# A two-layer decoder trunk in float32: one 512-column matmul for the high part of a weight in the up projections

## The chip, the cores and the metric
One core of a Trainium2 chip runs the whole program in one launch. The metric is the device time of one execution in microseconds (us); smaller is better. TensorE multiplies, VectorE (DVE in the profile) and ScalarE (ACT) do the elementwise work, GpSimd (POOL) nearly nothing here, and SyncE (SP) issues the DMAs.

## The reference
256 tokens of width 2048 pass two layers in float32. Each layer is `x <- LN(alpha*x + mixer(x))`, then `x <- LN(alpha*x + ConvFFN(x))`. The mixer of layer 0 is stick-breaking attention (8 heads of 128) beside RWKV-7 time mixing (16 heads of 64); that of layer 1 is gated linear attention (4 heads). The part that is changed is the feed-forward network:

```python
def conv_ffn(x, w_up, conv_w, conv_b, w_down):
    gate, up = jnp.split(x @ w_up, 2, axis=-1)          # 2048 -> 2 x 5632
    gate = causal_depthwise_conv(gate, conv_w) + conv_b # three taps along the tokens
    h = jax.nn.gelu(gate, approximate=False) * up
    return h @ w_down                                   # 5632 -> 2048
```

## The kernel before
Every product is made from float32r operands: a float32 number is split in a high part (its cast to float32r) and a low part (what is left), and a product is high x high + high x low + low x high, three matmuls that add up in one PSUM accumulator.

Weights come from HBM as granules of 128 x 512 (`Stream`): one DMA brings two, ScalarE casts the high part (line 56) and VectorE subtracts it from the raw weight for the low part (line 57). The split granules wait in a ring of tiles (four, with up to four more in some stages). TensorE's order is the order in which the program is written; the other engines' orders are set by a scheduler that knows dependencies and priorities, weights first.

There are two kinds of product. `gemm_b` (lines 180 to 188) keeps a weight tile of 128 x 128 in the array and streams 256 tokens past it: the accumulator holds 128 features x 256 tokens. A granule holds four k tiles of one feature tile, so four granules, 48 matmuls of 256 columns, make one feature tile. `gemm_a` (lines 192 to 197) keeps the activations in the array and streams 512 weight columns: the accumulator holds 128 tokens x 512 features. The mixers' input projections are mostly `gemm_b` by way of `tile_b`, the output and down projections `gemm_a` by way of `block_a` and `proj_out`. `wave` makes the first four feature tiles of a projection at once, because the normed activations come only piece by piece.

Accumulators come from two pools of four PSUM banks: `g` for the projections (4 buffers of one bank, line 115), `t` for the rest. One bank holds 512 float32 numbers a partition. `tile_b` uses half of a bank; in the up projection gate and up of a pair p share one bank.

What reads an accumulator depends on the place. In layer 0 `shift` reads it twice, on ScalarE (line 548) and on VectorE (line 549), for the RWKV tiles r, k and v; q and k of the attention are copied by ScalarE (lines 942, 944). In layer 1 `q_post` and `k_post` read it on VectorE (lines 1079, 1090, 1093), `gate` on ScalarE (line 1179, shown as line 157). `residual` reads the blocks of `proj_out` on VectorE (line 302). In the up projection `finish` does the convolution, the GELU and the product with up (lines 453 to 460). Work beside the products, such as the attention itself, runs in generators that take a step every few granules (`tick`).

The tile of the input is `[128, 2, 256]`: the high parts of one k tile for all tokens, then the low parts.

Of the kernel before, what the change touches and what calls it, by code (L numbers as in the profile page):

```python
# [18 lines left out]
# how many granules the steps of the work beside the products lie apart  # L19
# [3 lines left out]
class Stream:  # L23
    """Weight granules [128, 512] in the order of use, split into two float32r parts."""
# [7 lines left out]
    def ahead(self):  # L32
        """split the first four granules before those of the stream before have been used"""
        K = self.K
        K.wpos = 0
        self.ready = [self.make() for _ in K.wbase]
# [27 lines left out]
class Kern:  # L64
# [14 lines left out]
    # Work beside the products: a generator that yields the number of granules to let pass  # L79
    # before its next step.  # L80
# [28 lines left out]
    def pools(self, ctx):  # L109
        tc = self.tc  # L110
        e = ctx.enter_context
        self.cst = e(tc.tile_pool(name="cst", bufs=1))
        self.xp = e(tc.tile_pool(name="xp", bufs=16))
        self.sm = e(tc.tile_pool(name="sm", bufs=2))
        self.psg = e(tc.tile_pool(name="psg", bufs=4, space=bass.MemoryType.PSUM))
        self.pst = e(tc.tile_pool(name="pst", bufs=4, space=bass.MemoryType.PSUM))
# [4 lines left out]
    def wpools(self, ctx, n, nraw, nw):  # L121
        """weights arrive n granules at a time"""
# [5 lines left out]
    def wextra(self, ctx, n, start=0):  # L128
        """room for n more granules as long as ctx is open"""
# [6 lines left out]
    def rsqrt(self, x, y, t):  # L136
        """y = x^-1/2 by exp(-ln(x)/2) and one step of Newton; t is scratch"""
# [7 lines left out]
    # The table sets of ScalarE are loaded where act_set says: what needs a table is issued  # L145
    # behind its load, and a load behind what needs the set before it.
# [16 lines left out]

    def g(self, shape=(P, 512)):
        return self.psg.tile(list(shape), F32, tag="g", name=f"g{self.uid()}")
# [4 lines left out]
    def split(self, dst, src, eng_hi="act"):  # L170
        """dst [128, 2, n] float32r <- src in two parts"""
# [7 lines left out]
    # out[f, tok] += W[k, f] x[k, tok]; a granule holds 4 k tiles of one feature tile  # L179
    def gemm_b(self, ps, w, xT, kg):  # L180
        nc = self.nc
        for j in range(4):
            k = kg * 4 + j
            wh, wl = w[:, 0, j * P:(j + 1) * P], w[:, 1, j * P:(j + 1) * P]
            nc.tensor.matmul(ps, lhsT=wh, rhs=xT[k][:, 0], start=k == 0, stop=False)  # L185
# [4 lines left out]
    # out[tok, n] += x[k, tok] W[k, n], both in two float32r parts; a granule holds 512 columns  # L190
    # of one k tile
# [7 lines left out]
    # out[tok, n] += x[k, tok] W[k, n]; a granule holds 512 columns of one k tile  # L199
    def wave(self, st, xT, made=None, first=False):  # L200
        """four feature tiles at once, k outside; made: steps that give 2 k tiles each"""
        nc = self.nc
        ps = [self.g((P, S)) for _ in range(4)]
# [5 lines left out]
        def mm(a, w, k, part=None):  # L209
            j = k % 4  # L210
            wh, wl = w[:, 0, j * P:(j + 1) * P], w[:, 1, j * P:(j + 1) * P]
            if part != 1:
                nc.tensor.matmul(ps[a], lhsT=wh, rhs=xT[k][:, 0], start=k == 0, stop=False)  # L213
                nc.tensor.matmul(ps[a], lhsT=wl, rhs=xT[k][:, 0], start=False, stop=False)  # L214
            if part != 0:
                nc.tensor.matmul(ps[a], lhsT=wh, rhs=xT[k][:, 1], start=False, stop=k == KT - 1)  # L216
# [22 lines left out]
        return ps  # L239
# [7 lines left out]
    def block_a(self, st, xs):  # L247
        """512 columns, both halves of the tokens"""
# [9 lines left out]
    def proj_out(self, xs, st, done, then=None, tail=4, after=None):  # L258
        """xs: (high, low) halves per k tile and token half; done(m, nb, ps, columns)"""
        nc = self.nc  # L260
        n = len(xs)
        for nb in range(4):
# [5 lines left out]
            # the first half of the tokens ends ahead of the second, and that in two parts  # L268
# [64 lines left out]
    def norm_out(self, h, g_d, b_d, out):  # L333
        """the last norm: a job before the sums are complete, that gives what follows each half"""
# [4 lines left out]
        # the blocks of each half that ScalarE and GpSimd take  # L339
# [24 lines left out]
    def norm(self, h, stats, gcol, bcol, g_d, b_d, lp, bp, then):  # L364
        """h^T of the normed h in two float32r parts. Returns the tiles, the steps that give two
        of them each, and a job that ends the norm of h itself."""
# [71 lines left out]
    def ffn(self, h, stats, ln, st, down_d, cw_d, then=None, last=None):  # L438
        """cw [128, 44, 4]: three taps and the bias of each feature"""
        nc = self.nc  # L440
        with ExitStack() as ctx:
# [10 lines left out]
            def finish(p, g, u):  # L452
                c = cw[:, p]
                t = ft.tile([P, S], F32, tag="ct", name=f"ct{self.uid()}")
# [7 lines left out]
            ps = self.wave(st, xT, made)  # L462
            finish(0, ps[0], ps[1])
            finish(1, ps[2], ps[3])
            self.spawn(late)
            for p in range(2, NFF):
                ps = (self.t if p < 4 else self.g)((P, 2, S))
                for a in range(2):
                    for kg in range(4):
                        self.gemm_b(ps[:, a], st.next(), xT, kg)  # L470
                finish(p, ps[:, 0], ps[:, 1])
# [6 lines left out]
# host side: layout only  # L478
def gran_b(np, W, cols):
    """[n, 128, 4, 512]: per feature tile (128 columns from cols[i]), its 16 k tiles"""  # L480
# [8 lines left out]
def wave(np, g):  # L489
    """the first four tiles [4, 128, 4(kg), 512] with the k groups outside"""  # L490
# [5 lines left out]
def gran_a(np, W):  # L496
    """[nb * K/512, 128, 4, 512]: per 512 columns, its k tiles"""
# [33 lines left out]
class Mix0:  # L531
    """In-projection of layer 0, stick-breaking attention and RWKV-7 time mixing."""
# [18 lines left out]
    def run(self, xT, made, win_b, win_v, win_qk, lw_d, g2_d, open_h, outer):  # L551
# [6 lines left out]
        with ExitStack() as ctx:  # L558
# [101 lines left out]
            def k_post(p, k):  # L660
# [6 lines left out]
                # the norm's guard; the factor 2^20 keeps ln in its range  # L667
# [735 lines left out]
```

## Time and profile before

| | |
|---|---|
| time of three runs | 2438.54, 2439.29, 2439.73 us (median 2439.29) |
| span of the profiled execution | 2437.5 us (the page gives no time beside it) |
| TensorE busy | 2405.3 us, 99%, 17770 matmuls |
| VectorE busy | 1554.8 us, 64% |
| ScalarE busy | 1301.8 us, 53% |
| mean granted TensorE clock | 0.991 of full speed |
| matmuls of `gemm_b` from tiles x, of 256 columns (lines 185 to 187) | 3 x 3024 |

The page's busy time counts a matmul from its start to its end, 282 ns for one of 256 columns, though the next one starts long before; how often one starts in a stretch says what it costs. The up projection of layer 0 runs from about 600 to 1030 us, that of layer 1 from about 1700 to 2170; the mixer of layer 0 fills the first 440 us, that of layer 1 lies between 1300 and 1680 us with its output projection.

### The profile page before, as it was taken

Reading aid. Unit: us, or ns where it says so; the run is one execution under the profiler, and the core shown is the slowest. Engines: PE = TensorE matmul, PEld = TensorE weight load, DVE = VectorE, ACT = ScalarE, POOL = GpSimd, SP = SyncE. Lnnn points to the kernel's source line nnn. Section 1 sums busy time; section 2 is a strip of 40 time slices with the busy share of each in tenths; the row PEclk is TensorE's granted clock in tenths of the full one; section 3 lists DMA queues with packets and bytes.
Section 4 is the critical chain, followed back from the end, with each engine's and each line's share of the span. In section 5 each row is a group of like instructions: output and inputs, shape, how many; then the busy total and the mean of one; then the engine's idle time right before and its main releaser. Section 6 shows DMA issues by size and latency. Waiting matters only on the chain.

```text
span 2437.5 us, 44745 instructions
## 1 busy us (share of the span) xinstructions
PE 2405.3 (99%) x17770; PEld 2253.8 (92%) x17770; DVE 1554.8 (64%) x2847; ACT 1301.8 (53%) x2450; POOL 12.0 (0%) x14
## 2 busy tenths in 40 slices
PE   8999999999999999999999999999999999999997
PEld 7998988889999999988898998989999999998887
DVE  5887755677666666655558666667766666655555
ACT  6655555555555555544437555555555555554442
POOL 0000000000000000000000000000000000000001
PEclk9999998999999999999999999999999999999999
DMA  5444433656555555555555554564655555565553
GB/s 175 161 134 168 145 105 104 210 163 224 189 184 185 188 183 188 184 193 195 184 173 177 170 173 166 175 213 163 218 184 189 183 185 188 183 216 199 195 186 138
DMA packets 123698, 434.79 MB, mean 178 GB/s; under 512 B 13744, under 2 KB 14640, under 8 KB 123488
## 3 DMA queue, kind: packets, MB, share of 16 engines
q1 hardware_dynamic: 123488, 431.93, 52.7%
q8 instruction: 139, 2.28, 0.4%
q14 instruction: 71, 0.58, 0.1%
HBM read 429.77 MB, written 2.10 MB: 177 GB/s over the span
## 4 chain that ended last, share of the span: by engine, by line
PE 95%; DVE 3%; DMA 1%; ACT 1%; issue 0%; SPq 0%; DVEq 0%; ACTq 0%
PE g L185 17%; PE g L187 17%; PE g L186 17%; PE g L195 10%; PE g L196 10%; PE g L197 10%; PE t L197 1%; PE t L195 1%; PE t L196 1%; DMA raw<-w0b 1%; PE g L213 1%; PE g L216 1%; PE g L214 1%; PE t L185 1%; PE t L187 1%; PE t L186 1%
## 5 line engine op out<-in xcount | busy, mean ns | idle before, releaser
L57 DVE TENSOR_TENSOR w<-raw,w 128x512 fp32r<-128x512 f32 x1584 | 1080.1, 690 | 769.9 <-ACT w L56 766.4
L56 ACT CAST w<-raw 128x512 fp32r<-128x512 f32 x1584 | 965.6, 620 | 958.3 <-PE g L187 461.4
L185 PE MATMUL g<-x,w 128*128 128x256 f32 x3024 | 852.6, 282 | 0.0
L187 PE MATMUL g<-x,w 128*128 128x256 f32 x3024 | 852.1, 282 | 0.0
L186 PE MATMUL g<-x,w 128*128 128x256 f32 x3024 | 851.8, 282 | 0.0
L185 PEld LDWEIGHTS g<-x,w 128*128 128x128 f32 x3024 | 569.7, 188 | 0.2
L186 PEld LDWEIGHTS g<-x,w 128*128 128x128 f32 x3024 | 569.7, 188 | 0.3
L187 PEld LDWEIGHTS g<-x,w 128*128 128x128 f32 x3024 | 569.6, 188 | 0.0
L197 PE MATMUL g<-w,hT 128*128 128x512 f32 (+1 forms) x704 | 255.4, 363 | 0.0
L196 PE MATMUL g<-w,hT 128*128 128x512 f32 (+1 forms) x704 | 255.3, 363 | 0.0
L195 PE MATMUL g<-w,hT 128*128 128x512 f32 (+1 forms) x704 | 255.3, 363 | 0.0
L185 PE MATMUL g<-xi,w 128*128 128x256 f32 x608 | 179.2, 295 | 0.0
L187 PE MATMUL g<-xi,w 128*128 128x256 f32 x608 | 173.4, 285 | 3.0 <-DVE w L57 2.9
L186 PE MATMUL g<-xi,w 128*128 128x256 f32 x608 | 172.8, 284 | 0.0
L195 PEld LDWEIGHTS g<-w,hT 128*128 128x128 f32 x704 | 133.0, 189 | 20.7
L196 PEld LDWEIGHTS g<-w,hT 128*128 128x128 f32 x704 | 133.0, 189 | 20.5
L197 PEld LDWEIGHTS g<-w,hT 128*128 128x128 f32 x704 | 132.9, 189 | 20.5
L187 PEld LDWEIGHTS g<-xi,w 128*128 128x128 f32 x608 | 116.1, 191 | 3.8 <-DVE w L57 3.8
L185 PEld LDWEIGHTS g<-xi,w 128*128 128x128 f32 x608 | 116.2, 191 | 3.1 <-issue 1.5
L186 PEld LDWEIGHTS g<-xi,w 128*128 128x128 f32 x608 | 116.3, 191 | 0.8
L213 PE MATMUL g<-x,w 128*128 128x256 f32 x192 | 55.8, 298 | 0.0
L157 ACT ACTIVATE ct<-ct 128x256 f32<-128x256 f32 x88 | 36.8, 418 | 32.5 <-DVE ct L457 32.5
(316 smaller groups left out, 2852.2 us busy)
## 6 DMA issues: line engine op xcount, KB each, us to landing
raw<-up SPq DMA_DIRECT2D x352, 512.0 KB, 3.6
raw<-dn SPq DMA_DIRECT2D x176, 512.0 KB, 4.3
raw<-w0b SPq DMA_DIRECT2D x53, 512.0 KB, 3.6
raw<-w1b SPq DMA_DIRECT2D x40, 512.0 KB, 3.8
raw<-w0qk SPq DMA_DIRECT2D x32, 512.0 KB, 3.6
raw<-w0o SPq DMA_DIRECT2D x32, 512.0 KB, 4.2
raw<-w1v SPq DMA_DIRECT2D x32, 512.0 KB, 3.6
raw<-w1o SPq DMA_DIRECT2D x32, 512.0 KB, 4.4
```

Source lines behind the costliest of these rows:

```text
L56: i = nc.scalar.copy(out=w[:, 0], in_=src).ins
L57: K.split_ins = nc.vector.tensor_sub(out=w[:, 1], in0=src, in1=w[:, 0].bitcast(F32)).ins
L157: i = self.nc.scalar.activation(out=out, in_=in_, func=func, **kw).ins
L185: nc.tensor.matmul(ps, lhsT=wh, rhs=xT[k][:, 0], start=k == 0, stop=False)
L186: nc.tensor.matmul(ps, lhsT=wh, rhs=xT[k][:, 1], start=False, stop=False)
L187: nc.tensor.matmul(ps, lhsT=wl, rhs=xT[k][:, 0], start=False, stop=k == KT - 1)
L195: nc.tensor.matmul(ps, lhsT=xh, rhs=w[0], start=first, stop=False)
L196: nc.tensor.matmul(ps, lhsT=xh, rhs=w[1], start=False, stop=False)
L197: nc.tensor.matmul(ps, lhsT=xl, rhs=w[0], start=False, stop=last)
L213: nc.tensor.matmul(ps[a], lhsT=wh, rhs=xT[k][:, 0], start=k == 0, stop=False)
L214: nc.tensor.matmul(ps[a], lhsT=wl, rhs=xT[k][:, 0], start=False, stop=False)
L216: nc.tensor.matmul(ps[a], lhsT=wh, rhs=xT[k][:, 1], start=False, stop=k == KT - 1)
```

## The change
In the up projections the accumulator of a feature tile becomes a whole bank of 512 columns. The high part of a weight tile meets the high and the low part of x in one matmul of 512 columns: the first 256 columns of the bank collect high x high, the others high x low. The low part of the weight meets the high part of x in a matmul of 256 columns, into the first half. At the end `finish` copies the second halves of gate and up to SBUF with ScalarE and adds the first halves with VectorE, and works on that sum. In `wave` the first four k tiles still take three matmuls, because the low parts of x come later.

A pair (gate, up) now needs two banks. So the pool `g` is made of two tiles of two banks each. `g2` gives such a tile; `g`, which all other products use, gives one half of a tile and at the next call the other.

```diff
-        self.psg = e(tc.tile_pool(name="psg", bufs=4, space=bass.MemoryType.PSUM))
+        self.psg = e(tc.tile_pool(name="psg", bufs=2, space=bass.MemoryType.PSUM))
+        self.half = None
...
+    def g2(self):
+        self.half = None
+        return self.psg.tile([P, 2, 512], F32, tag="g", name=f"g{self.uid()}")
+
     def g(self, shape=(P, 512)):
-        return self.psg.tile(list(shape), F32, tag="g", name=f"g{self.uid()}")
+        if self.half is None:
+            t = self.g2()
+            self.half = t[:, 1]
+            b = t[:, 0]
+        else:
+            b, self.half = self.half, None
+        return b[:, 0:math.prod(shape[1:])]
...
     def gemm_b(self, ps, w, xT, kg):
+        wide = ps.shape[1] == 2 * S
...
+            if wide:
+                nc.tensor.matmul(ps, lhsT=wh, rhs=xT[k].rearrange("p a b -> p (a b)"), start=k == 0, stop=False)
+                nc.tensor.matmul(ps[:, 0:S], lhsT=wl, rhs=xT[k][:, 0], start=False, stop=k == KT - 1)
+                continue
...
     def wave(...):
+            if wide and part is None:
+                nc.tensor.matmul(ps[a], lhsT=wh, rhs=xT[k].rearrange("p a b -> p (a b)"), start=False, stop=False)
+                nc.tensor.matmul(ps[a][:, 0:S], lhsT=wl, rhs=xT[k][:, 0], start=False, stop=k == KT - 1)
+                return
...
-            def finish(p, g, u):
+            def finish(p, ps):
+                gu = ft.tile([P, 2, S], F32, tag="gu", name=f"gu{self.uid()}")
+                if isinstance(ps, list):
+                    for i in range(2):
+                        nc.scalar.copy(out=gu[:, i], in_=ps[i][:, S:])
+                        nc.vector.tensor_add(out=gu[:, i], in0=ps[i][:, 0:S], in1=gu[:, i])
+                else:
+                    nc.scalar.copy(out=gu, in_=ps[:, :, S:])
+                    nc.vector.tensor_add(out=gu, in0=ps[:, :, 0:S], in1=gu)
+                g, u = gu[:, 0], gu[:, 1]
...
             for p in range(2, NFF):
-                ps = (self.t if p < 4 else self.g)((P, 2, S))
+                ps = [self.t(), self.t()] if p < 4 else self.g2()
```

Three places show how the order moves. The first is TensorE in the mixer of layer 0, from the RWKV tile r2 to the tile k4. Before, r2 is the accumulator g_1076 and k4 is g_1192; x is `xi`.

```order
L185 MATMUL g_1076<-xi_99,w_1171 128x256
L186 MATMUL g_1076<-xi_99,w_1171 128x256
L187 MATMUL g_1076<-xi_99,w_1171 128x256
L185 MATMUL g_1192<-xi_84,w_1195 128x256
L186 MATMUL g_1192<-xi_84,w_1195 128x256
L187 MATMUL g_1192<-xi_84,w_1195 128x256
```

The next tile starts without a wait. After the change both tiles are halves of g_1072 (the names do not tell the halves apart; the row that waits is the first of k4):

```order
L205 MATMUL g_1072<-xi_99,w_1167 128x256
L206 MATMUL g_1072<-xi_99,w_1167 128x256
L207 MATMUL g_1072<-xi_99,w_1167 128x256
L205 MATMUL g_1072<-xi_84,w_1190 128x256 [waits DVE_49]
L206 MATMUL g_1072<-xi_84,w_1190 128x256
L207 MATMUL g_1072<-xi_84,w_1190 128x256
```

The first matmul of k4 now waits for VectorE. What it waits for is the read of r2 by `shift` (L587 after the change), which stands in VectorE's order here:

```order
L57 TENSOR_TENSOR w_1222<-raw_1220,w_1222 128x512 [waits DMAHW3_49,Activation_49]
L706 TENSOR_SCALAR e_1149<-t_1147 128x256 [waits PE_49]
L721 TENSOR_TENSOR PB<-PB,E_558 64x4x64
L57 TENSOR_TENSOR w_1237<-raw_1220,w_1237 128x512 [waits Activation_49]
L143 SCALAR_TENSOR_TENSOR e_1150<-e_1150,e_1149 128x256 [waits DVE_49,Activation_49]
L587 SCALAR_TENSOR_TENSOR e_1182<-g_1072,vec,e_1182 128x255 [waits Activation_49]
```

The read itself waits for ScalarE, which reads the accumulator first. Nothing of this moved within VectorE's queue; new is that TensorE waits for its last row. In all, 37 places where an accumulator of `g` begins in the second half of a tile have such a wait: 11 behind `shift` and 8 behind a q of the attention in layer 0, 8 behind q or k and 7 behind a gate in layer 1, and 3 at blocks of its output projection. The last kind looks so, from one block of layer 1's `proj_out` to the next, in TensorE's order:

```order
L216 MATMUL g_16409<-w_16644,oT_15512 128x512 [waits DVE_49]
L217 MATMUL g_16409<-w_16644,oT_15512 128x512
L215 MATMUL g_16492<-w_16644,oT_15512 128x512
L216 MATMUL g_16492<-w_16644,oT_15512 128x512
L217 MATMUL g_16492<-w_16644,oT_15512 128x512
L215 MATMUL g_16492<-w_16662,oT_15497 128x512 [waits DVE_49,Activation_49]
L216 MATMUL g_16492<-w_16662,oT_15497 128x512
```

Here the second token half of one block and the first token half of the next share g_16492, because an odd number of tiles was taken before; the row with two waits is the first of the next block, and its wait on VectorE is for the reading of the block before.

In the up projection three rows for a weight tile become two:

```order
L202 MATMUL g_6695<-x_5808,w_6698 128x512 [waits DVE_49,Activation_49]
L203 MATMUL g_6695<-x_5808,w_6698 128x256 [waits DVE_49]
L202 MATMUL g_6695<-x_5809,w_6698 128x512
L203 MATMUL g_6695<-x_5809,w_6698 128x256
L202 MATMUL g_6695<-x_5810,w_6698 128x512
```

The first row's wait on VectorE is for the addition of the pair two before. TensorE has 2784 matmuls fewer in all.

## Rows read from the trace of the kernel before

**Rows 1.** The page's chain that ended last, shares of the span by engine.
```profile
PE 95%; DVE 3%; DMA 1%; ACT 1%; issue 0%; SPq 0%; DVEq 0%; ACTq 0%
```

**Rows 2.** Table of stretches, up and down projection: PE, PEld, DVE, ACT, POOL busy, PEclk, DMA.
```profile
700.00:1000.00 300.00, 300.00 (x2531) 300.00 (x2530) 185.79 (x318) 162.41 (x291) 0.00 (x0) 1.00 0.55 186
...
2200.00:2300.00 100.00, 100.00 (x443) 82.85 (x442) 53.48 (x80) 45.60 (x74) 0.00 (x0) 1.00 0.57 195
```

**Rows 3.** VectorE's groups by line in 700 to 1000 us: count, busy us, mean ns, idle.
```profile
L57 DVE TENSOR_TENSOR w<-raw,w 128x512 fp32r<-128x512 f32 x211 | 145.9, 692 | 114.0 <-ACT w L56 114.0
```

**Rows 4.** Timeline, a cast out of PSUM on ScalarE: start us, us, instruction.
```profile
1333.20 0.58 ACT L174 CAST vs<-g 128x512 fp32r<-128x512 f32 x1
```

**Rows 5.** Timeline, from an RWKV tile r to the next tile, three engines.
```profile
150.73 0.28 PE L187 MATMUL g<-xi,w 128*128 128x256 f32 x1
150.85 0.28 PE L185 MATMUL g<-xi,w 128*128 128x256 f32 x1
...
151.42 0.60 ACT L56 CAST w<-raw 128x512 fp32r<-128x512 f32 x1
151.93 0.41 ACT L141 ACTIVATE e<-e 128x256 f32<-128x256 f32 x1
152.25 0.46 ACT L548 ACTIVATE e<-g,omm 128x256 f32<-128x256 f32 x1
...
152.66 0.42 DVE L142 SCALAR_TENSOR_TENSOR e<-e,e 128x256 f32<-128x256 f32 x1
153.00 0.48 DVE L549 SCALAR_TENSOR_TENSOR e<-g,vec,e 128x255 f32<-128x255 f32 x1
```

**Rows 6.** Timeline, behind an RWKV tile v.
```profile
217.16 0.40 PE L195 MATMUL g<-w,xi 128*128 128x512 f32 x1
...
218.68 0.48 DVE L549 SCALAR_TENSOR_TENSOR e<-g,vec,e 128x255 f32<-128x255 f32 x1
```

**Rows 7.** Timeline, behind a q tile of the attention in layer 0.
```profile
246.15 0.28 PE L185 MATMUL g<-xi,w 128*128 128x256 f32 x1
...
246.88 0.37 ACT L942 COPY e<-g 128x256 f32<-128x256 f32 x1
```

**Rows 8.** Timeline, behind a later q tile, with TensorE's own wait there.
```profile
271.26 0.28 PE L185 MATMUL g<-xi,w 128*128 128x256 f32 x1
...
274.71 0.37 ACT L942 COPY e<-g 128x256 f32<-128x256 f32 x1
...
274.53 0.38 PE L187 MATMUL g<-xi,w 128*128 128x256 f32 x1 [1.45 <-DVE w L57]
```

**Rows 9.** Timeline, behind a q tile beside the RWKV chain.
```profile
341.27 0.36 ACT L942 COPY e<-g 128x256 f32<-128x256 f32 x1
...
341.71 0.39 PE L185 MATMUL g<-xi,w 128*128 128x256 f32 x1
```

**Rows 10.** Timeline, behind a k tile of layer 1.
```profile
1349.76 0.28 PE L185 MATMUL g<-x,w 128*128 128x256 f32 x1
...
1350.30 0.42 DVE L1093 TENSOR_TENSOR kd<-g,e 128x256 f32<-128x256 f32 x1
```

**Rows 11.** Timeline, behind a gate tile of layer 1.
```profile
1527.22 0.28 PE L185 MATMUL g<-x,w 128*128 128x256 f32 x1
...
1528.00 0.47 ACT L157 ACTIVATE e<-g,vec 128x256 f32<-128x256 f32 x1
```

**Rows 12.** Timeline, from one block to the next in layer 1's output projection.
```profile
1605.97 0.39 PE L195 MATMUL g<-w,oT 128*128 128x512 f32 x1
...
1606.09 1.28 DVE L302 SCALAR_TENSOR_TENSOR h<-h,g 128x512 f32<-128x512 f32 x2
```

**Rows 13.** Timeline, a pause of TensorE behind `shift` and its end.
```profile
180.47 0.47 DVE L549 SCALAR_TENSOR_TENSOR e<-g,vec,e 128x255 f32<-128x255 f32 x1
...
181.09 0.52 PE L723 MATMUL t<-ct,e 128*128 128x128 f32 x3 [2.51 <-DVE e L751]
```

**Rows 14.** Table of stretches around that pause: PE busy, PEclk, DMA share, GB/s.
```profile
175.00:180.00 5.00, 3.58 (x31) 1.00 0.34 105
```

More of the change, by code (lines that the diff above doesn't have):

```diff
@@ L197, in gemm_a, with wave @@
         nc.tensor.matmul(ps, lhsT=xl, rhs=w[0], start=False, stop=last)
-    def wave(self, st, xT, made=None, first=False):
+    def wave(self, st, xT, made=None, first=False, wide=False):
         nc = self.nc
-        ps = [self.g((P, S)) for _ in range(4)]
+        if wide:
+            pp = [self.g2() for _ in range(2)]
+            ps = [p[:, i] for p in pp for i in range(2)]
+        else:
+            ps = [self.g((P, S)) for _ in range(4)]
         def step():
@@ L211, in mm @@
             wh, wl = w[:, 0, j * P:(j + 1) * P], w[:, 1, j * P:(j + 1) * P]
+            if wide and part is None:
+                nc.tensor.matmul(ps[a], lhsT=wh, rhs=xT[k].rearrange("p a b -> p (a b)"), start=False, stop=False)
+                nc.tensor.matmul(ps[a][:, 0:S], lhsT=wl, rhs=xT[k][:, 0], start=False, stop=k == KT - 1)
+                return
+            ph = ps[a][:, 0:S]
             if part != 1:
-                nc.tensor.matmul(ps[a], lhsT=wh, rhs=xT[k][:, 0], start=k == 0, stop=False)
-                nc.tensor.matmul(ps[a], lhsT=wl, rhs=xT[k][:, 0], start=False, stop=False)
+                nc.tensor.matmul(ph, lhsT=wh, rhs=xT[k][:, 0], start=k == 0, stop=False)
+                nc.tensor.matmul(ph, lhsT=wl, rhs=xT[k][:, 0], start=False, stop=False)
             if part != 0:
-                nc.tensor.matmul(ps[a], lhsT=wh, rhs=xT[k][:, 1], start=False, stop=k == KT - 1)
+                nc.tensor.matmul(ps[a][:, S:] if wide else ph, lhsT=wh, rhs=xT[k][:, 1], start=False, stop=k == KT - 1)
         step()
@@ L238, in wave @@
                     step()
-        return ps
+        return pp if wide else ps
     def tile_b(self, st, xT, make=None):
@@ L450, in ffn @@
             hT = [hTp.tile([P, 2, S], F32R, tag="hT", name=f"hT{self.uid()}") for _ in range(NFF)]
-            def finish(p, g, u):
+            def finish(p, ps):
                 c = cw[:, p]
+                gu = ft.tile([P, 2, S], F32, tag="gu", name=f"gu{self.uid()}")
[3 more added lines that the diff above has]
+                        nc.vector.tensor_add(out=gu[:, i], in0=ps[i][:, 0:S], in1=gu[:, i])
+                else:
+                    nc.scalar.copy(out=gu, in_=ps[:, :, S:])
+                    nc.vector.tensor_add(out=gu, in0=ps[:, :, 0:S], in1=gu)
+                g, u = gu[:, 0], gu[:, 1]
                 t = ft.tile([P, S], F32, tag="ct", name=f"ct{self.uid()}")
@@ L460, in finish @@
                 self.split(hT[p], t)
-            ps = self.wave(st, xT, made)
-            finish(0, ps[0], ps[1])
-            finish(1, ps[2], ps[3])
+            for p, ps in enumerate(self.wave(st, xT, made, wide=True)):
+                finish(p, ps)
             self.spawn(late)
             for p in range(2, NFF):
-                ps = (self.t if p < 4 else self.g)((P, 2, S))
+                ps = [self.t(), self.t()] if p < 4 else self.g2()
                 for a in range(2):
                     for kg in range(4):
-                        self.gemm_b(ps[:, a], st.next(), xT, kg)
-                finish(p, ps[:, 0], ps[:, 1])
+                        self.gemm_b(ps[a] if p < 4 else ps[:, a], st.next(), xT, kg)
+                finish(p, ps)
             stats = self.new_stats()
```

## The prediction
> **What bounds the kernel now.** I read the chain of waits first: TensorE holds 95% of it [rows 1], so only what changes TensorE's own time counts. Then the table of stretches [rows 2]. In the up projection the granted clock is 1.00 and 2531 matmuls of 256 columns take 300 us, 118.5 ns from one to the next; in the down projection 443 of 512 columns take 100 us, 225.7 ns. In both stretches TensorE is busy throughout while VectorE and ScalarE have slack. Last I read, place by place, the timeline around the moment when one accumulator is finished and the next begins. There the reader is to see two times: when the next accumulator's first matmul starts, and when the last reader of the old one ends. Today these have nothing to do with each other.
>
> **The shorter product (gain).** 256 extra columns cost 225.7 - 118.5 = 107.2 ns, and 107.2 for 256 columns is 2.39 per ns. So a 256-column matmul is 107.2 ns of columns and 11.3 ns that do not depend on them. Before, a weight tile takes 3 x 118.5 = 355.5 ns; after, 225.7 + 118.5 = 344.2 ns, 11.3 ns less. Merged are 88 feature tiles x 16 k tiles of each layer, less the 4 tiles x 4 k tiles in which `wave` still issues three: 1392 a layer, 2784 in all. 2784 x 11.3 ns = 31.5 us, all on the path.
> No row shows a 512-column matmul alternating with one of 256. Bound on the good side: the short one follows for its columns alone, 107.2 ns, and the tile saves 22.6 ns, 63 us in all. Bound on the bad side: the 11.3 ns stay with the weight change and nothing is saved. I take the middle, since both shapes carry nearly the same fixed part (225.7 - 2 x 107.2 = 11.3).
> The Trainium skill ("TensorE: Matmul & The Clock Gate", section "Wait — 56ns, not 53.3ns?") puts the fixed cost of a warm matmul at about 2.5 ns. By it the gain would be 2784 x 2.5 ns = 7 us. The two stretches of [rows 2] disagree, with 11.3 ns.
>
> **The halves added afterwards (hidden).** Each of 88 pairs gets a ScalarE copy of 128x512 out of PSUM and a VectorE addition of 128x512. Nearest rows: a 128x512 cast out of PSUM, 0.58 us [rows 4], and the 128x512 subtraction, 0.69 us [rows 3]. A pair takes 32 x 344 ns = 11.0 us. From [rows 2], ScalarE is busy 162.41/300 and VectorE 185.79/300, so 6.2 and 7.0 us of an 11.4 us pair; they become 6.7 and 7.7 us of 11.0. TensorE stays the bound. With two double-bank buffers instead of four single ones, pair p + 2 waits for the addition of pair p, which has a whole pair (11 us) to be done. Cost taken: 0. Were that cover gone, it would show as a wait once per pair, and 88 waits of 1 us would cost 88 us.
>
> **The shared tile (loss).** This is not in the up projection at all. `g` now hands out halves of a two-bank tile, and the order above shows what follows: the first matmul into the second half waits for the last reader of the first half, though it writes another bank. Before, four separate tiles left every reader three tiles of time. Nothing of TensorE's stands between the two, so TensorE stands still from the time that the next accumulator would have started until the reader ends. I counted these places in the new order and priced each by the same place in the trace of before, reader's end less next start:
> - `shift` behind tiles r0 to r6 of layer 0: the weight copy for the ring, a second ScalarE operation and the ScalarE read come first, then VectorE's read ends at 153.48 against a start at 150.85: 2.63 us [rows 5]. 7 x 2.63 = 18.4 us.
> - `shift` behind v0, v2, v4, v6: 219.16 - 217.16 = 2.00 us [rows 6]. 4 x 2.00 = 8.0 us.
> - q of the eight stick-breaking heads (a ScalarE copy): 247.25 - 246.15 = 1.10 us [rows 7], two such; two longer, one 275.08 - 271.26 = 3.82 us [rows 8], the other taken as 3.0. Of the four that lie beside the RWKV chain, chain matmuls stand between and cover the copy in three (it ends at 341.63, the tile starts at 341.71, [rows 9]); one taken as 1.2. Sum 10.2 us. Behind a long one TensorE today waits 1.45 us for weights [rows 8], which it would not do again; for this and its like I take off 2.7: 7.5 us.
> - q and k of layer 1, eight places: 1350.72 - 1349.76 = 0.96 us for k [rows 10], q about the same. 7.7 us.
> - gates of layer 1, behind r tiles 3, 5, 7, 9, 11, 13, 15: 1528.47 - 1527.22 = 1.25 us [rows 11]. 7 x 1.25 = 8.8 us.
> - Those 13 tiles are an odd number, so `proj_out` starts in the second half of a tile, and three of its blocks start behind the reading of the block before: two 128x512 operations of VectorE end at 1607.37, the block starts at 1605.97: 1.40 us [rows 12]. 4.2 us.
> Sum 54.6 us. A matmul that waited starts up to 0.15 us behind the reader's end (181.09 against 180.94, [rows 13]); 34 open waits x 0.1 = 3.4 us. Loss: 58.0 us.
> The bounds of this term: if each reader went first in its queue, as it may when TensorE stands and the queues run empty, the 2.63 become about 1.6 (0.62 + 0.46 + 0.48 of [rows 5]) and the others lose a third: about 40 us. With the restart at 0.25 us and some places that lie behind a backlog of VectorE, about 72 us. Below 40 it could only come if the reads took less time than they do.
> The three last blocks with halves also share a tile between the two token halves, but 12 matmuls (1.4 us) lie between there; 0.
> The Trainium skill ("PSUM — Partial Sum Buffer", section "Summary: rules for kernel authors") tells to read PSUM in another bank than the one being written, and to guard by bank. By this rule the two banks need no wait at all and the loss would be 0; but it is the program's order that holds the wait here, so the rule changes no chance.
>
> **Sum.** The page gives a span of 2437.5 us; the three runs have a median of 2439.3, so 1.8 us lie around the span. 2437.5 - 31.5 + 58.0 = 2464.0 for the span, 2465.8 with what lies around it: about 2466 us, 1.1% slower.
>
> **Rivals.**
> A. The alternating shapes save the full 22.6 ns and the readers go first: -63 + 40 = -23, 2416 us. This is the way to faster: it needs weight loads that never hold up a short matmul. For it: a load has 225 ns to hide behind. Against: the same fixed 11.3 ns at both widths. It decides once the saving passes 20.8 ns a tile at 58 us of loss, or 14.4 at 40.
> B. The waits cost little, since what stands still now would have stood later: -31.5 + 10 = 2418 us. For it: 2.7 us of such waits exist in [rows 8] and near it. Against: TensorE is busy without a break in nearly all of the stretches of these places, so there is little to pay them from.
> C. The product does not get shorter, because the fixed cost is that of a weight change or of the columns' start and comes back elsewhere: 2439.3 + 58 = 2497 us. By the 2.5 ns of the Trainium skill's page on TensorE, named above, it would be 2490 us.
> D. The pauses lower the granted clock. Each tile behind a pause that ran at half speed would cost some 6 us; 10 of them 60 us, 2526 us. Against: a pause of 2.51 us [rows 13] lies in a stretch with a granted clock of 1.00 [rows 14], and the new ones are shorter or alike.
>
> **How the numbers follow.** Forecast 80%. A 5%, B 6%, C 6%, D 3%. The forecast's own range is 2439.3 + 40 - 35 to 2439.3 + 72 - 25, that is 2444 to 2486; cases C and D lie above, A and B below. I take 2444 to 2490, a little above the forecast's own end since two of the four rivals lie there; it leaves out about 0.2. The measurement tells 0.2%, 5 us, from no change. Faster than 2434: A, most of B and a sliver of the forecast with a larger saving, 0.11. Within: the rest of these and the forecast's low end, 0.08. Slower: 0.81.
>
> **What would show each step.** In the profile after: two matmuls a weight tile in the up projection at 344 ns for the two, which is 581 matmuls in 100 us. VectorE at about 70% there and no TensorE wait for the addition. In the list of waits, TensorE waiting for the readers in `shift`, q and k, the gate and `residual`, 1 to 2.6 us each, some 34 times, 50 to 60 us in sum, none of which stands in the list of before. The mixers grow by these sums, layer 0 by about 34 us, layer 1 with its output projection by 21. Wrong would be: TensorE idle under 35 us (B), 333 ns or less a weight tile (A), 355 (C), or a granted clock under 1.00 in the stretches of the mixers where it was 1.00 (D).

## The result and the profile after

| | median us | lowest to highest | runs |
|---|---|---|---|
| before | 2439.51 | 2438.54 to 2442.56 | 4 |
| after | 2499.82 | 2496.64 to 2506.32 | 4 |

The ratio is 1.0248, 95% interval 1.0232 to 1.0264: 60 us slower. The prediction said 2466 us, 2444 to 2490. The side is right, the size is not, and the time lies above the range. The profiled execution has a span of 2504.5 us; its own time, 2506.32, is the highest of the four.

The page after, first its busy times, then the chain that ended last, which answers to [rows 1]:

```profile
PE 2419.3 (97%) x14986; PEld 2133.6 (85%) x14986; DVE 1612.6 (64%) x2939; ACT 1358.2 (54%) x2542; POOL 12.0 (0%) x14
...
PE 89%; DVE 5%; ACT 3%; DMA 1%; issue 1%; SPq 0%; ACTq 0%; DVEq 0%
```

TensorE held 95% of the chain before and holds 89% now; VectorE and ScalarE have 8% of it instead of 4%. The up projection, in the stretch of [rows 2], and the timeline there (start us, duration us, instruction):

```profile
700.00:1000.00 300.00, 300.00 (x1710) 262.90 (x1709) 202.79 (x347) 179.50 (x320) 0.00 (x0) 1.00 0.56 187
```

```profile
799.88 0.39 PE L202 MATMUL g<-x,w 128*128 128x512 f32 x1
800.10 0.28 PE L203 MATMUL g<-x,w 128*128 128x256 f32 x1
800.22 0.40 PE L202 MATMUL g<-x,w 128*128 128x512 f32 x1
800.46 0.28 PE L203 MATMUL g<-x,w 128*128 128x256 f32 x1
800.58 0.40 PE L202 MATMUL g<-x,w 128*128 128x512 f32 x1
```

1710 matmuls are 855 weight tiles in 300 us, 351 ns each, and the timeline repeats it: 0.70 us for two tiles. The forecast was 344. VectorE is at 68% and ScalarE at 60%, and TensorE never stops.

TensorE's waits, longest sums first (engine, line, whom it waited for: us, times, longest):

```profile
PE g L205 <- DVE e L587: 24.3, 11, 2.9
PE g L205 <- ACT e L980: 9.1, 5, 4.6
PE g L205 <- ACT e L158: 6.9, 6, 1.2
...
PE g L205 <- DVE qd L1117: 4.6, 4, 2.1
PE g L215 <- DVE h L331: 4.1, 3, 1.4
PE g L205 <- DVE kd L1131: 3.8, 4, 0.9
...
PE g L215 <- ACT e L158: 1.1, 1, 1.1
```

L587 is the VectorE read of `shift`, L980 the copy of q, L158 the gate, L1117 and L1131 q and k of layer 1, L331 the residual. These rows make 34 waits and 53.9 us, which is the list that the prediction gave. Two of them: a pause behind an r tile, which answers to [rows 5], and the long one behind a q tile, which answers to [rows 8]:

```profile
126.42 0.60 ACT L56 CAST w<-raw 128x512 fp32r<-128x512 f32 x1
127.24 0.45 ACT L586 ACTIVATE e<-g,omm 128x256 f32<-128x256 f32 x1
127.99 0.47 DVE L587 SCALAR_TENSOR_TENSOR e<-g,vec,e 128x255 f32<-128x255 f32 x1
...
128.53 0.38 PE L205 MATMUL g<-xi,w 128*128 128x256 f32 x1 [2.50 <-DVE e L587]
```

```profile
320.44 0.52 ACT L158 ACTIVATE e<-e 128x384 f32<-128x384 f32 x1
320.86 1.12 ACT L56 CAST w<-raw 128x512 fp32r<-128x512 f32 x2
321.89 0.36 ACT L980 COPY e<-g 128x256 f32<-128x256 f32 x1
322.30 0.58 PE L205 MATMUL g<-xi,w 128*128 128x256 f32 x1 [4.64 <-ACT e L980]
```

In the second the copy of q stands in ScalarE's queue behind four steps of a softplus (the last of them L158 at 320.44), a cast of an attention output and two weight casts (L56), and TensorE stands with it. Nor does the clock always stay at the 1.00 of [rows 14]. Three stretches of layer 0 with pauses (columns of [rows 2]; the last are granted clock, DMA share, GB/s):

```profile
105.00:185.00 80.00, 67.46 (x548) 64.94 (x548) 58.34 (x140) 41.61 (x87) 1.20 (x1) 1.00 0.36 119
205.00:215.00 10.00, 7.66 (x61) 6.88 (x59) 9.82 (x18) 4.30 (x10) 0.00 (x0) 1.00 0.38 122
215.00:225.00 10.00, 8.10 (x43) 7.73 (x43) 4.63 (x13) 3.00 (x6) 0.00 (x0) 0.66 0.29 94
```

In the first, five pauses of 2.5 us behind r tiles left the clock at 1.00. In the second TensorE was idle for 2.34 of 10 us, and it went on at 1.2 instead of 2.4 GHz for part of the third. The clock also fell behind two pauses of only 1.9 us, at 235 and 252 us. So the length of a pause alone doesn't decide.

Lengths of the stages in us, read from TensorE's timelines (the kernels to the right are those of the experiments). Layer 0 counts from its first matmul to where its output projection runs on undisturbed (447.9 us before). The up projection counts from where its `wave` runs on undisturbed (543.8 and 1694.2 us before) to the first matmul of the down projection. The mixer of layer 1 counts from the end of the down projection, its output projection to the end of its own last matmul. Last row: the lower clock in layer 0's mixer, as the sum of (1 - granted clock) x 5 us over the table of 5 us stretches. It takes every us at half clock as half lost, so it is the most that the clock can have taken. In each of the five kernels 13 to 16 us of it lie beside the RWKV chain, in the last 100 us of the stage.

| | before | after | again | halves only | four banks |
|---|---|---|---|---|---|
| layer 0 up to its output projection | 442.2 | 496.3 | 488.9 | 488.0 | 441.9 |
| up projection, each layer, without the start of `wave` | 487.1 | 480.4 | 480.4 | 487.1 | 480.4 |
| mixer of layer 1 with the norm | 310.2 | 333.3 | 332.8 | 333.7 | 310.2 |
| its output projection | 88.5 | 93.5 | 93.4 | 93.5 | 88.5 |
| lower clock in layer 0's mixer | 15.4 | 35.9 | 27.3 | 27.4 | 13.7 |

The down projections keep their 243.1 us in all of them.

### The profile page after: what moved, and what is told of

Same layout as the page of the kernel before. It is cut to its first block, busy times and chain, and to the rows that moved or that the text cites. A ratio compares the mean times of both kernels' runs of the same rounds, so it can differ in the third digit from the quotient of the medians.

```text
span 2504.5 us, 39507 instructions
## 1 busy us (share of the span) xinstructions
PE 2419.3 (97%) x14986; PEld 2133.6 (85%) x14986; DVE 1612.6 (64%) x2939; ACT 1358.2 (54%) x2542; POOL 12.0 (0%) x14
## 4 chain that ended last, share of the span: by engine, by line
PE 89%; DVE 5%; ACT 3%; DMA 1%; issue 1%; SPq 0%; ACTq 0%; DVEq 0%
PE g L202 24%; PE g L203 12%; PE g L215 9%; PE g L217 9%; PE g L216 9%; PE g L205 5%; PE g L207 4%; PE g L206 4%; DVE w L57 2%; ACT w L56 2%; PE t L216 1%; PE t L202 1%; PE t L217 1%; PE t L215 1%; DMA raw<-w0b 1%
## 5 line engine op out<-in xcount | busy, mean ns | idle before, releaser
L56 ACT CAST w<-raw 128x512 fp32r<-128x512 f32 x1584 | 968.3, 621 | 938.2 <-PE g L203 320.0
L202 PE MATMUL g<-x,w 128*128 128x512 f32 x2560 | 898.9, 393 | 0.0
L203 PE MATMUL g<-x,w 128*128 128x256 f32 x2560 | 724.1, 283 | 0.0
L202 PEld LDWEIGHTS g<-x,w 128*128 128x128 f32 x2560 | 480.7, 188 | 111.1
L203 PEld LDWEIGHTS g<-x,w 128*128 128x128 f32 x2560 | 481.3, 188 | 0.0
L205 PE MATMUL g<-xi,w 128*128 128x256 f32 x608 | 186.3, 306 | 33.4 <-DVE e L587 24.3
L206 PE MATMUL g<-xi,w 128*128 128x256 f32 x608 | 177.5, 292 | 0.0
L207 PE MATMUL g<-xi,w 128*128 128x256 f32 x608 | 177.3, 292 | 0.0
L205 PEld LDWEIGHTS g<-xi,w 128*128 128x128 f32 x608 | 121.4, 200 | 40.5 <-DVE e L587 26.5
L205 PE MATMUL g<-x,w 128*128 128x256 f32 x464 | 133.4, 287 | 15.2 <-ACT e L158 6.9
L206 PE MATMUL g<-x,w 128*128 128x256 f32 x464 | 131.6, 284 | 0.0
L207 PE MATMUL g<-x,w 128*128 128x256 f32 x464 | 131.4, 283 | 0.0
L206 PEld LDWEIGHTS g<-xi,w 128*128 128x128 f32 x608 | 121.8, 200 | 0.9
L207 PEld LDWEIGHTS g<-xi,w 128*128 128x128 f32 x608 | 121.1, 199 | 0.0
L205 PEld LDWEIGHTS g<-x,w 128*128 128x128 f32 x464 | 88.2, 190 | 18.1 <-ACT e L158 8.1
```

Of the source, the lines that this page charges most:

```text
L56: i = nc.scalar.copy(out=w[:, 0], in_=src).ins
L202: nc.tensor.matmul(ps, lhsT=wh, rhs=xT[k].rearrange("p a b -> p (a b)"), start=k == 0, stop=False)
L203: nc.tensor.matmul(ps[:, 0:S], lhsT=wl, rhs=xT[k][:, 0], start=False, stop=k == KT - 1)
L206: nc.tensor.matmul(ps, lhsT=wh, rhs=xT[k][:, 1], start=False, stop=False)
L207: nc.tensor.matmul(ps, lhsT=wl, rhs=xT[k][:, 0], start=False, stop=k == KT - 1)
```

## The experiments

Each kernel has line numbers of its own. The theory after reading both traces: the product gives back 13.4 us, and all the rest is the shared tile, partly through waits and partly through a clock that falls behind them.

**Four tiles of one bank each, with the wide product.**

```diff
-        self.psg = ...(name="psg", bufs=2, ...)
+        self.psg = ...(name="psg", bufs=4, ...)
     def g2(self):
-        return self.psg.tile([P, 2, 512], F32, tag="g", ...)
+        return [self.g(), self.g()]
     def g(self, shape=(P, 512)):
-        ... the halves of a two-bank tile ...
+        return self.psg.tile(list(shape), F32, tag="g", ...)
```

> The wide products of the change, but g hands out four tiles of one bank each, as before; a pair uses two of them. Theory (sharing theory): all of the loss, the lower granted clock of layer 0's mixer too, comes from accumulators that share a tile; the wide product itself saves what the up projection shows after the change, 478.6 to 472.05 us in each layer, 13.2 us, and about 1 us in wave. So 2439.5 - 14 = 2425 us, with no wait of TensorE for shift, q, k, gate and residual, and the granted clock of the mixers as in the kernel before. By the term of the prediction (11.3 ns a weight tile) it would be 2408 us. Rival (other causes): a good part of the waits or of the lost clock comes from the wide products or their added operations; then 2435 us or more, and waits or a lower clock stay.

Measured: 2427.51 us against 2441.15, ratio 0.9941 (0.9928 to 0.9955). The top of the list of TensorE's waits, both of which before has too (5.8 and 5.7 us), and the stretch in which the changed kernel's clock fell:

```profile
PE t L408 <- DVE h L398: 5.8, 6, 1.7
PE g L235 <- ACT xi L180: 5.0, 1, 5.0
```

```profile
180.00:250.00 70.00, 69.81 (x479) 62.98 (x480) 52.75 (x118) 39.25 (x81) 0.00 (x0) 1.00 0.51 173
```

The new waits are gone, the clock is 1.00, and 13.6 us remain as gain. All of the loss hangs on the sharing, and this version beats both kernels.

**The sharing alone, with the narrow product.** The kernel before, with

```diff
+    def g2(self): ...   # a tile [P, 2, 512], two of them
     def g(self, shape=(P, 512)):
+        ... first half, then second half of one g2 ...
-                ps = (self.t if p < 4 else self.g)((P, 2, S))
+                ps = self.t((P, 2, S)) if p < 4 else self.g2()[:, 0].rearrange(...)
```

> The narrow products of the kernel before, but g hands out the two halves of two-bank tiles (the up projection's pairs each take a whole such tile and use its first half). Sharing theory: layer 0 up to its output projection grows by the 53 us seen after the change (some 33 us of waits, the rest a lower granted clock that follows them), layer 1 with its output projection by 28: 2439.5 + 75 to 81 = 2514 to 2520 us. By the prediction's own terms (waits of 58 us, clock untouched): 2497 us. Rival (other causes): the clock falls for another reason, then layer 0 grows by 33 us only and the granted clock of its mixer is that of before: about 2500 us.

Measured: 2514.0 us, ratio 1.0309 (1.0289 to 1.0330), 73 us more than before. Its waits and its clock:

```profile
PE g L196 <- DVE e L561: 25.0, 11, 2.9
PE g L196 <- ACT e L954: 9.2, 5, 4.7
PE g L196 <- ACT e L158: 6.9, 6, 1.2
```

```profile
205.00:215.00 10.00, 7.09 (x37) 6.89 (x38) 6.37 (x19) 3.83 (x9) 0.00 (x0) 0.68 0.42 142
```

The same waits and the same falls of the clock without one wide matmul. The theory's 2514 holds, at its low end: layer 0 grew by 45.8 us (488.0 - 442.2) and not by 53. 2500 and the prediction's own 2497 are too low.

**A tile of its own for each accumulator, still only two tiles.**

```diff
     def tile_b(self, st, xT, make=None):
+        self.half = None
     def block_a(self, st, xs):
+        self.half = None
```

> The changed kernel with one edit: tile_b and block_a begin a fresh two-bank tile each time, so that no accumulator shares its tile with the one before; there are still two such tiles. Sharing theory: the reader of a tile has the whole next tile (5.7 us and more) for itself, the waits go, about as four separate banks: 2425 us, up to 2430 where a reader lies behind a backlog. Rival (two buffers instead of four): it is the number of tiles that costs, the wait only moves one tile on; then 2450 us or more with waits for the same readers.

Measured: 2430.39 us, ratio 0.9959 (0.9945 to 0.9972). Two lines take nearly all of the loss away (four banks is 2.9 us faster still). It is not the number of tiles; it is who is the neighbour in one. This trace also holds the pause of [rows 13], which is not of the sharing's making. It is 2.56 us long here, and behind it the clock did fall:

```profile
180.00:185.00 5.00, 3.49 (x19) 3.15 (x20) 4.84 (x15) 1.20 (x4) 0.00 (x0) 0.77 0.57 203
```

The kernel before kept 1.00 behind the same pause. One pause in one execution doesn't tell what the clock does behind pauses of its length.

**No copy and no addition.** As four banks, with the second halves left out of the result:

```diff
-    nc.scalar.copy(out=gu[:, i], in_=ps[i][:, S:])
-    nc.vector.tensor_add(out=gu[:, i], in0=ps[i][:, 0:S], in1=gu[:, i])
-    g, u = gu[:, 0], gu[:, 1]
+    g, u = ps[0][:, 0:S], ps[1][:, 0:S]
```

> As e1, but the second halves are neither copied by ScalarE nor added by VectorE: the product of the weights' high part and x's low part is computed and left out of the result. Theory (hidden): the copy and the addition cost nothing, the time is that of e1 within 2 us and a weight tile takes the same 351 ns. Rival: their reads of PSUM or their shares of the engines are what keeps the weight tile at 351 instead of 344 ns; then 2688 x 7 ns = 19 us less than e1.

Measured: 2426.52 us, ratio 0.9942 (0.9928 to 0.9956); the interval is that of four banks. The stretch of the up projection, first with the addition, then without:

```profile
700.00:1000.00 300.00, 300.00 (x1711) 262.94 (x1710) 204.56 (x374) 182.84 (x348) 0.00 (x0) 1.00 0.57 188
```

```profile
700.00:1000.00 300.00, 300.00 (x1711) 262.95 (x1710) 188.46 (x320) 164.67 (x294) 0.00 (x0) 1.00 0.56 187
```

VectorE and ScalarE lose 16 and 18 us of work, TensorE does the same 1711 matmuls. Hidden, as forecast.

**Four wide, then four short.** As four banks, with

```diff
         for j in range(4):
             matmul(ps, lhsT=wh, rhs=xT[k] (both parts), ...)
-            matmul(ps[:, 0:S], lhsT=wl, rhs=xT[k][:, 0], ...)
+        for j in range(4):
+            matmul(ps[:, 0:S], lhsT=wl, rhs=xT[k][:, 0], ...)
```

> As e1, but within a granule of four k tiles the four wide matmuls are issued first and the four short ones behind them (not in wave). After the change a wide one takes 230 ns and a short one 121, 351 the pair, where stretches of one shape alone show 225.7 and 118.5, 344. Theory F (the change of shape costs): one change of shape per four weight tiles is left, three quarters of the 7 ns go: 2624 x 5 = 13 us less than e1, about 2414 us. Theory W (each short matmul has to hide a weight load, and what of the load it can't hide is left over): the number of short ones is the same, so nothing changes: 2427 us, 351 ns per weight tile.

Measured: 2426.59 us against 2444.98 for before, ratio 0.9939 (0.9922 to 0.9957); 1710 matmuls in the same 300 us. Nothing gained: theory F as it was put falls.

**The changed kernel with its pauses filled.**

```diff
     def tile_b(self, st, xT, make=None, fill=0):
+        if fill and make is None and self.half is not None:
+            w, f = self.last, self.t((P, S))
+            for i in range(fill):
+                nc.tensor.matmul(f, lhsT=w[:, 0, 0:P], rhs=xT[0][:, 0], start=True, stop=True)
```

> The changed kernel with matmuls that nobody reads put where TensorE stands still in layer 0's mixer, into another PSUM tile: 20 of 256 columns (2.4 us) ahead of each r and k tile that lies in a second half, 15 (1.8 us) ahead of v, 8 (0.95 us) ahead of q. They fill the pauses without moving their ends. Theory (the pauses lower the clock): the stretches at 0.5 behind pauses, at 215 to 260 and 320 to 327 us of the profile after, go to 1.00, which gives back 7 to 9 us, and up to 20 if those at 55 to 75 and 90 to 100 go as well: 2481 to 2493 us against 2500. Rival (the clock falls by the half-used matmuls of the chains beside, not by the pauses): the same stretches stay at 0.5 and the time is 2500 us or more, since the fillers take up to 1 us each beyond the pauses.

And beside it on the same chip **the change again**:

> The changed kernel again, to see which of its stretches at half clock return: those behind pauses at 215 to 260 and 320 to 327 us should, by the theory that the pauses lower the clock; the one of 17 us at 55 to 73, which the kernel with halves only didn't have, need not. Without it the span is about 2496 us instead of 2504.5.

Measured: 2488.12 us filled (ratio 1.0183, 1.0167 to 1.0199), 2501.02 us again (1.0237, 1.0219 to 1.0254). The stretch of the v tiles, first filled, then again:

```profile
205.00:245.00 40.00, 39.46 (x318) 37.38 (x317) 27.22 (x62) 21.66 (x50) 0.00 (x0) 1.00 0.42 142
```

```profile
205.00:245.00 40.00, 33.81 (x233) 31.38 (x230) 24.30 (x60) 19.25 (x43) 0.00 (x0) 0.87 0.40 132
```

The work that nobody reads makes the kernel 12.9 us faster. Theory and sign are right, the pauses do lower the clock. Besides the falls that the kernel before has too, it falls in the change again at 86.6, 209.5, 230.0, 247.0 and 315.3 us, each time beside a pause, for 3.4 or 6.8 us; the first profile after and the halves alone show the same five falls. At the first four, which the fillers covered, the falls are gone. The fifth, at a q copy, kept its fall (granted clock 0.66 in 305 to 310 us): TensorE still waited 3.4 us there, which 0.95 us of filling didn't cover.

Not all of the gain is the clock. Both traces hold the same 2256 matmuls of layer 0's input projections. Followed matmul by matmul, the change again falls behind by 1.5, 2.7, 1.5 and 1.5 us in the four falls, some 7 us in all. About 0.3 us more comes at most of the filled pauses, also where the clock is 1.00 in both, since the fillers did move the ends of the pauses, which the expectation had excluded:

```profile
118.70 2.53 PE L275 MATMUL t<-xi,w 128*128 128x256 f32 x20
...
121.27 0.62 ACT L56 CAST w<-raw 128x512 fp32r<-128x512 f32 x1 [1.10 <-PE t L275]
```

They hold a weight tile of the ring for longer, so ScalarE's cast of the next weights comes behind the read in `shift` instead of ahead of it. The next tile starts 2.49 us behind the last product here (118.58 to 121.07), and 2.80 in the change again (118.95 to 121.75).

The change again doesn't have the long fall: in 55 to 75 us it shows 1.00, where the first profile after shows 0.57. So some 8.5 us of that profile's 35.9 belong to that execution. The span of the change again, 2497.1, fits the median of the first result.

**The products alone.** Stretches of matmuls without any wait, in one execution at a granted clock of 1.00, for example the third and the fifth:

```python
for i in range(2 * N): mm(A, lhsT=hi(i), rhs=xx(i))          # 512 columns
for i in range(N):                                           # the pair of the change
    mm(A, lhsT=hi(i), rhs=xx(i)); mm(A[:, 0:S], lhsT=lo(i), rhs=xh(i))
```

> Not the computation: stretches of matmuls alone, operands ready, nothing waiting, the output is what they leave. In order: 96 wide to warm up; 96 triples as in the kernel before; 192 of 512 columns; 192 of 256; 96 pairs 512/256 as in the change; the same with the short one in another bank; the same with one weight for both; groups of four and four; 192 of 256 with one weight; 192 of 128; 192 of 384. The term of the prediction: the pairs take 344 ns and the 351 of the kernel come from its surroundings. Theory F: the pairs take 351, the groups of four 346. Theory W: the pairs take 351 with either bank and either weight, the groups of four too, and 128 columns take well over the 65 ns that 107.2 ns per 256 and a fixed 11.3 would give, because the load doesn't fit behind them.

The groups by line, count, shortest, median and longest duration in ns, then the first and last start, from which a stretch's length is read (its first start to that of the next row). Order: triples, 512, 256, pairs, other bank, one weight, four and four, 256 with one weight, 128, 384:

```profile
L1378 PE MATMUL ga<-x,w x96: 277/283/283, 35.4 to 69.6; 128*128 128x256 f32 x96
L1382 PE MATMUL ga<-x,w x192: 389/389/397, 70.0 to 113.3; 128*128 128x512 f32 x192
L1384 PE MATMUL ga<-x,w x192: 277/283/283, 113.5 to 136.5; 128*128 128x256 f32 x192
L1386 PE MATMUL ga<-x,w x96: 395/398/403, 136.6 to 170.1; 128*128 128x512 f32 x96
L1389 PE MATMUL ga<-x,w x96: 395/398/403, 170.5 to 204.1; 128*128 128x512 f32 x96
L1392 PE MATMUL ga<-x,w x96: 395/398/403, 204.4 to 238.0; 128*128 128x512 f32 x96
L1396 PE MATMUL ga<-x,w x96: 387/396/398, 238.3 to 271.3; 128*128 128x512 f32 x96
L1400 PE MATMUL ga<-x,w x192: 283/283/283, 272.0 to 294.9; 128*128 128x256 f32 x192
L1402 PE MATMUL ga<-x,w x192: 224/274/280, 295.1 to 316.3; 128*128 128x128 f32 x192
L1404 PE MATMUL ga<-x,w x96: 334/334/388, 316.4 to 349.4; 128*128 128x384 f32 x96
```

(The expectations of the next study took these from finer starts, hence their last digits.) 512 columns take (113.5 - 70.0)/192 = 226.6 ns, 256 take 120.3, so one of each would be 346.9. The pair takes (170.5 - 136.6)/96 = 353.1, with the other bank and with one weight the same, in groups of four 351.0. The product costs 351 to 353 by itself; the prediction's 344 is reached in none of these orders. And 128 columns take 110.9 ns, where 107.2 ns per 256 columns and 11.3 fixed would give 64.9: below 256 columns something else than the columns sets the pace.

**Half the weights.** The same, again in one execution, with `lhsT` cut to 64 columns in one or both of the pair:

```diff
-            mm(A, lhsT=hi(i), rhs=xx(i))
+            mm(A[0:64], lhsT=hi(i)[:, 0:64], rhs=xx(i))
             mm(A[:, 0:S], lhsT=lo(i), rhs=xh(i))
```

> Not the computation: stretches of matmuls alone again, to see where the 6.6 ns come from that a pair of 512 and 256 columns takes beyond the stretches of one shape (353.3 against 226.8 + 119.9). In order: 96 of 512; 96 pairs 512/256 as control; pairs in which the wide one has weights of 64 instead of 128 columns (a smaller load behind the short one); pairs in which the short one has; pairs in which both have; then all with 64 columns of weights: 192 of 128 columns, 192 of 256, 192 of 512; then pairs 512/384 and 512/128 with full weights. Theory L (the weight load behind a short matmul doesn't fit): the first kind of narrow pair takes 347 ns or less, the second 353; 128 columns take clearly less than the 111.5 ns of full weights. Theory F (a change of width costs, whatever is loaded): both kinds stay at 353 and 512/384 takes some 6 ns more than 226.8 + 175.2 = 402.

Order: pairs, pairs with the wide one's weights halved, with the short one's, with both; then halved weights with 128, 256 and 512 columns; 512/384 and 512/128:

```profile
L1378 PE MATMUL ga<-x,w x96: 389/398/403, 35.4 to 68.9; 128*128 128x512 f32 x96
L1381 PE MATMUL ga<-x,w x96: 389/389/395, 69.3 to 101.6; 128*64 128x512 f32 x96
L1384 PE MATMUL ga<-x,w x96: 391/392/392, 101.9 to 134.9; 128*128 128x512 f32 x96
L1387 PE MATMUL ga<-x,w x96: 388/388/397, 135.2 to 167.5; 128*64 128x512 f32 x96
L1390 PE MATMUL ga<-x,w x192: 220/222/225, 167.9 to 179.3; 128*64 128x128 f32 x192
L1392 PE MATMUL ga<-x,w x192: 274/276/280, 179.4 to 201.1; 128*64 128x256 f32 x192
L1394 PE MATMUL ga<-x,w x192: 387/390/398, 201.2 to 245.1; 128*64 128x512 f32 x192
L1396 PE MATMUL ga<-x,w x96: 396/398/398, 245.3 to 284.6; 128*128 128x512 f32 x96
L1399 PE MATMUL ga<-x,w x96: 398/442/447, 285.0 to 317.3; 128*128 128x512 f32 x96
```

128 columns fall from 110.9 to (179.4 - 167.9)/192 = 59.9 ns: there the weight load set the pace. In the pair, half the load behind the short matmul (the wide one's weights) takes 353.1 to 339.6 ns; half the load behind the wide one gives 346.9. So theory L is borne out for the load that the short matmul has to cover, 13.5 ns of the pair. It doesn't explain all: it said 353 for the second kind, and 512/384, where no matmul is short, takes (285.0 - 245.3)/96 = 413.5 ns against 226.6 + 173.7 = 400.3 from the stretches of one shape (384 columns: (349.4 - 316.4)/95 for two). Theory F said some 6 ns more there, and it is 13. With 512/128 it is (317.3 - 285.0)/95 = 340.0 against 226.6 + 110.9 = 337.5. Alternating widths cost something that the load's size doesn't tell. What that is stays open.

## Why the prediction was wrong in size

Its own steps, by the change again (span 2497.1, near the median), where 59.6 us were added to the span:

- **The shared tile: right.** Forecast 58.0 us of waits. Layer 0's mixer grew by 46.7 us, at most 11.9 of them clock (27.3 - 15.4); layer 1 with its output projection by 27.5, 1.7 of them clock (0.66 in 1380 to 1385 us). That leaves 60.6 us, at the places that were priced. Layer 0 has 34.8 where 34 and its part of the 3.4 stood. Layer 1 has 25.8 for 21. The restart was priced too low there: from one gate tile to the next the kernel needs 1.41 us more than before, of which 1.14 are the wait, so 0.27 go beside it where 0.1 stood. The first q waited 1.7 us for 0.96, and three `mix` products, which were not on the list, waited up to 0.5 us behind `v_block`. Rival B, waits that are paid from others, did not come. (The 0.62 us in this term's lower bound is 0.60 in [rows 5], which moves nothing.)
- **The shorter product: the step that failed first.** "I take the middle, since both shapes carry nearly the same fixed part (225.7 - 2 x 107.2 = 11.3)." One matmul fewer was to save this 11.3 ns. It saved 6.7 us a layer, 13.4 for 31.5, that is 4.8 ns a tile. The equality that was leaned on is no evidence: 107.2 is the difference of the two prices, so what is left over comes out the same at both widths whatever the prices are. They were right for stretches of one shape, but a price per matmul can't be carried into a mixture: the pair takes 353.1 ns alone, where its shapes take 346.9 apart. Part of the cause is shown: the load of the wide matmul's weights has to be covered by the short matmul ahead of it, and half that load takes 13.5 ns off the pair. Rival A had looked at the other load, which has the wide matmul's 225 ns to hide behind. Why the mixture costs more than its parts is not shown beyond that, since 512/384 does so too. A hint stood in the row that was used: with 256 columns the loads (second column) were busy for 300.00 of 300 us, with 512 for 82.85 of 100. The short matmul was at the edge of its load already (113.5 ns with half the weights, 120.3 with all). The Trainium skill ("TensorE: Matmul & The Clock Gate", section "LDWEIGHTS (loading the stationary operand)") gives a load about its columns divided by 1.2 in ns, an estimate of 107 ns for 128 columns and 53 for 64; the 110.9 and 59.9 ns of the products alone agree to within 7 ns. By that estimate a load lasts as long as the 107.2 ns that the prediction gave to 256 columns, which is why the row deserved a look. By the 2.5 ns of fixed cost that the prediction quoted from the Trainium skill the gain would have been 7 us, by the 11.3 ns 31.5; the 13.4 measured lie between.
- **The clock: rival D, underrated at 3%.** It was argued away from one pause that left the clock at 1.00 [rows 13, 14]. For the five pauses of 2.5 us behind r tiles that argument held. Behind others it didn't, shorter ones too: 12 us at most in the change again, 20 in the profile after. What tells the ones from the others stays open. D's price, 6 us a tile, was too high; the four falls that the filling took away had cost 1.5 to 2.7 us each.
- **The halves added afterwards: right**, at nothing, and VectorE at 68% as forecast.

The sum of the misses: 18.1 (31.5 - 13.4) + 11.9 + 1.7 + (60.6 - 58.0) = 34 us, against 2499.8 - 2466 = 34. If the clock took less than its most, the waits took as much more, and the sum stays. The range would have held either of the two failures alone, not both. Rival C's 2497 us comes closest, for a reason that isn't its own: the product did get shorter, and the lower clock took as much away.

## What to carry to other kernels

Slices of one tile are one thing to a scheduler that tracks tiles: whoever writes the second half waits for who reads the first, so give each accumulator its own tile, or start a fresh one where the reader is late. Price a matmul in the mixture in which it will stand, with the weight load that it has to cover, and look at the load's busy share of the stretch that the price comes from. If waits are added to TensorE, count the clock that falls behind them as well as the waits, and don't take one pause that left it alone as proof for all.

## What was not expected of the hardware

- Useless matmuls in TensorE's pauses made a kernel 12.9 us faster, some 7 us of it because the granted clock behind them stayed at 1.00 (0.87 without them in 205 to 245 us).
- The length of a pause doesn't tell whether the clock falls: five of 2.5 us left it at 1.00, two of 1.9 us were followed by half clock.
- A matmul with 128 columns of moving data is hardly cheaper than one with 256: 110.9 against 120.3 ns, as long as each brings 128 columns of weights.
- Equal weights in successive matmuls save nothing: 120.3 ns with one weight throughout, 120.3 with changing ones.
- A wide matmul with half the weights isn't faster in a stretch of its own, (245.3 - 201.2)/192 = 229.7 ns against 226.6, though in the pair the halved load is worth 13.5 ns.
